# New layouts for the heads and tails of a decoder's feed-forward blocks, and for the opening of its sparse attention

## The chip, the cores and the metric

The kernel runs on one core of a Trainium2 chip. The metric is the device time of one execution in microseconds; lower is better. Runs of the kernel before gave 2072.43, 2068.01 and 2056.33 us, and their median is the time to compare with.

## What is computed

Two layers work on x (512 tokens of 1024 features, fp32). Each layer is a half-step gated feed-forward network (FFN), a mixer, and a second half-step FFN. The mixer of the first layer is a short gated convolution, that of the second is native sparse attention (NSA). Each of the six sub-layers starts from its own RMS norm with a shift and a scale, and its result is added to x through a gate. Shift, scale and gate come from the condition c. Cut to what matters:

```python
def adaln(x, g, shift, scale):
    return rms_norm(x, g) * (1 + scale[:, None, :]) + shift[:, None, :]

def swiglu(h, w_in, w_out):                        # 1024 -> 2 x 2816 -> 1024
    g, u = jnp.split(h @ w_in, 2, axis=-1)
    return (jax.nn.silu(g) * u) @ w_out

def short_conv_mixer(h, w_in, conv_w, w_out):      # 1024 -> 3 x 1024 -> 1024
    b_gate, c_gate, v = jnp.split(h @ w_in, 3, axis=-1)
    y = causal_conv_of_3(c_gate * v, conv_w)
    return (b_gate * y) @ w_out

def nsa_mixer(h, ...):     # 16 heads of 64, 4 groups of keys and values
    q, kc, vc, ks, vs, kw, vw, gl = jnp.split(h @ w_in, offs, axis=-1)
    q, k_sel, k_win = per-head rms_norm of q, ks, kw
    k_cmp = rms_norm(compress(kc)); v_cmp = compress(vc)   # blocks of 32, stride 16, gelu MLP
    out = sum over three branches of gate * softmax(q k^T + bias) v
    return out @ w_out
```

## The kernel before

**Data.** x lies transposed in SBUF: eight tiles x[d] of 128 features by 512 tokens. D is 1024, KD = 8 is the number of such tiles, T = 512, HT = 256; HALVES are the token columns 0 to 255 and 256 to 511. A matrix product has fp32 accuracy through three products: each operand is split into hi and lo (split, L165: ACT writes hi, then VectorE subtracts and writes lo), and mm3 (L169) adds hi x hi, hi x lo and lo x hi into one accumulator. So L170, L171 and L172 carry most of the matmuls, and L166 and L167 most of the splits. Weights are loaded as wraw by SP and split into whi and wlo (weights, L174). The default pool wp has three buffers of each; own gives another pool.

**Order.** The program is written stage by stage, and the tile scheduler puts each engine's instructions in an order by priority and dependence. Work under tc.high_priority() goes to the front of what is ready in its engine's order. At run time every engine then works strictly through its own list, and an instruction that waits holds all those behind it. SP issues loads, in its own order, and a load waits until the buffer that it writes is free.

**Stages**, with the microseconds of the profile: the first FFN, which also computes shifts, scales and gates (0 to 405), conv (to about 590), FFN2 (to 955), FFN3 (to 1314), NSA (to 1700), and FFN5 (to 2055).

**A norm.** Class Norm (L210) belongs to the sub-layer that it feeds. The residual of the sub-layer ahead adds to x[d], then square (L217) takes the square on ACT and sums it in nacc. When all eight d of a half are in, finish (L235) turns the sum by a matmul with ones into a column per token, takes the root in small VectorE steps (rsqrt, L192: eleven operations on 128x2 or 128x8), makes a diagonal dg (L249) and spreads it with another matmul pr (L250). Then piece (L293) makes h for one d and one half: xr = x * pr on VectorE (L297), hhi on ACT with scale and shift (L299), the full value hf or hfull by ACT (odd d, L302) or VectorE (even d, L304), and hlo as their difference on VectorE (L305).

**A head** is where a stage starts to use h piece by piece. head_start (L333) multiplies three weights with the first halves as the pieces come, then the fourth weight (L346 on), then the second halves in the same way. **A tail** (L359) is the end of a stage: its last outputs are computed in two halves of 256 columns, so that the norm of the first half can begin while the second is computed.

**FFN2, FFN3 and FFN5** use ffn (L460). The 22 hidden tiles come in three blocks (FOUR). For the first two hidden tiles the products are plain; the third is a plain pair; all later ones go through seven_products, a seven-multiplication scheme on 2 x 2 blocks. It needs four combinations t0 to t3 of quarters of hfull, split into th and tl (quarters, L307), and combinations qa and qb of the weight's quarters. p1 = the copy of its first product (L512); L518 to L524 combine the others into e, with the silu between, and keep splits e into ahi and alo. The last block's output products run over d = 0 and 1 in full width and over d = 2 to 7 in tail. Its weights come from in_ffo.

**conv** (L564) has three weights per output column tile: gate, value, b.

**NSA** (L639) starts with the compressor (L759): head_start over the key and value columns of the compressed branch, then sixteen ACT copies t (L779), the sum with positions flr (L788), its split flh and fll, the products ph, a gelu and a second product. Between those, natural (L658) makes queries and keys in natural layout (tokens on partitions) and normed gives each half its own root chain over 128x8. attend (L857) then goes through 32 units (group, head, branch) three deep. heads and keys turn queries and keys by transposes (pq and pk), table (L881) loads rows of the bias table by 32 issues of SP before the first unit, and the remaining projections are spread through the units. At the end the output projection of groups 2 and 3 loads four blocks er, splits them into eh and el, and adds its results in two halves.

**PSUM** has 8 banks. Before, every stage kind has its own layout: new_psum closes the pool and opens another with other tags (L64 to L75):

```python
BANKS = {"mm": 6, "pr": 2, "pre": 5, "pt": 3, "nat": 2, "s": 2, "t": 2, "o": 2}
def new_psum():
    nonlocal ps
    ps_stack.pop_all().close()
    ps = pool(ps_stack, "ps", 1, space=PSUM)
```

Of the kernel before, what the change touches and what calls it, by code (L numbers as in the profile page):

```python
# [11 lines left out]
F32 = mybir.dt.float32  # L12
F32R = mybir.dt.float32r
# [7 lines left out]
P = 128  # L21
# [12 lines left out]
NG = 4  # L34
# [17 lines left out]
def decoder_kernel(ctx, tc, xT, cT, ng, adaw, adab, ffi, ffo, cwi, cw, cwo,  # L52
# [13 lines left out]
    ps = None  # L66
    BANKS = {"mm": 6, "pr": 2, "pre": 5, "pt": 3, "nat": 2, "s": 2, "t": 2, "o": 2}

    def psum(name, tag="mm"):
        return ps.tile([P, T], F32, name=name, tag=tag, bufs=BANKS[tag])  # L70

    def new_psum():
        nonlocal ps
        ps_stack.pop_all().close()
        ps = pool(ps_stack, "ps", 1, space=PSUM)  # L75
# [98 lines left out]
    def weights(src, nk, ncol, own=None, held=3):  # L174
        def part(name, dt, bufs):
            return (own or wp).tile([P, nk * ncol], dt, name=name, tag=name, padded_shape=[P, KD * P], bufs=bufs)

        hi, lo = part("whi", F32R, held), part("wlo", F32R, held)
        raw = part("wraw", F32, 3 if own is None else 2)
# [30 lines left out]
    class Norm:  # L210
# [69 lines left out]
        def alloc(self, hp):  # L280
            self.full = None
            self.hi = [hp.tile([P, T], F32R, name=f"hhi{d}") for d in range(KD)]
            self.lo = [hp.tile([P, T], F32R, name=f"hlo{d}") for d in range(KD)]
# [3 lines left out]
        def alloc_seven(self, tt, tq):  # L287
            self.full = tq.tile([P, KD, T], F32, name="hfull")
            self.t = [tq.tile([P, KD // 2, HT], F32, name=f"t{j}") for j in range(4)]
# [3 lines left out]
        def piece(self, d, hf):  # L293
            a, b = HALVES[hf]
            sc, sh = mod(self.s, 0, d), mod(self.s, 1, d)
            xr = tmp("xr", HT, "xr")
            nc.vector.tensor_mul(xr, x[d][:, a:b], self.pr[hf][:, 0:HT])  # L297
            hi = self.hi[d][:, a:b]
            nc.scalar.activation(hi, xr, AF.Identity, scale=sc, bias=sh)  # L299
# [5 lines left out]
            nc.vector.tensor_tensor(self.lo[d][:, a:b], hf_, hi, ALU.subtract)  # L305

        def quarters(self):  # L307
            n = KD // 2
# [24 lines left out]
    def head_start(nrm, h, jobs, both=3):  # L333
        os = [psum("hs") for _ in jobs]

        def go(n, ks, a, b):
            for k in ks:
                w, wc, kw = jobs[n](k)
                project(os[n][:, a:b], w, wc, h, [(kw, k)], k == 0, k == KD - 1, a, b)

        with tc.high_priority():
            for d in range(KD):
                nrm.piece(d, 0)
        for k in range(KD):
            for n in range(both):
                go(n, [k], 0, HT)  # L346
        for n in range(both, len(jobs)):
            go(n, range(KD), 0, HT)
        for d in range(KD):
            nrm.piece(d, 1)  # L350
        for k in range(KD):
            for n in range(both):
                go(n, [k], HT, T)
        for n in range(both, len(jobs)):
            go(n, range(KD), HT, T)
        return os


    def tail(s, nrm, jobs, h, ahead):  # L359
        nxt = ahead() if ahead else None  # L360
        for a, b in HALVES:
            for d, w, wc, ks in jobs:
                o = psum("ty")
                project(o[:, 0:b - a], w, wc, h, ks, True, True, a, b)
                residual(s, d, o, nrm, a, b, True)
# [94 lines left out]
    def ffn(s, f, nrm, nxt, w0, ahead):  # L460
        with ExitStack() as es:
            hp = pool(es, "hp", 1)
            h = nrm.alloc(hp)
            in_es = es.enter_context(ExitStack())
            tt = pool(in_es, "tt", 1)
            swa = pool(in_es, "swa", 1)
# [780 lines left out]
```

## Time and profile before

| | us |
|---|---|
| runs | 2072.43, 2068.01, 2056.33; median 2068.01 |
| profiled execution: time | 2060.89 |
| its span, first to last instruction | 2058.8 |
| mean granted clock of TensorE in it | 0.988 |
| TensorE (PE) busy, 12404 matmuls | 1980.4 |
| VectorE (DVE) busy, 2634 instructions | 1505.2 |
| ScalarE (ACT) busy, 1361 instructions | 874.3 |
| GpSimd (POOL) busy, 395 instructions | 266.9 |

The page of the profile lists, by part, how busy each engine is, the chain that ended last, the costliest groups of instructions and the loads. A group's row names a line of the code, the engine, the tiles (out <- in), shape and count; then busy time, mean duration of one in ns, and the idle time of the engine just before them with what ended it. Matmuls overlap: one of 512 columns shows 0.39 to 0.40 us, while the next begins after 0.23. Waits are also answered by stretches of the span, and so are busy time and the granted clock.

### The profile page before, as it was taken

What the parts mean: (1) busy time and instruction counts of PE and PEld (TensorE: products, weight loads), DVE (VectorE), ACT (ScalarE), POOL (GpSimd) and SP (SyncE); (2) the same over time, 40 slices, a digit from 0 to 9 for tenths busy, and PEclk for the clock granted to TensorE, in tenths of its full rate; (3) what the DMA queues carried; (4) which work ended last, traced back from release to release, by engine and by line L of the source; (5) the groups of instructions that cost most, each with busy time, mean ns of one, the idle gap of its engine ahead of it and who ended that gap; (6) DMA issues with size and microseconds to landing.
All of it is one profiled execution on the core that took longest, in us unless ns stands there. A gap on an engine that the chain in (4) does not pass through costs nothing.

```text
span 2058.8 us, 32164 instructions
## 1 busy us (share of the span) xinstructions
PE 1980.4 (96%) x12404; PEld 1771.8 (86%) x12404; DVE 1505.2 (73%) x2634; ACT 874.3 (42%) x1361; POOL 266.9 (13%) x395
## 2 busy tenths in 40 slices
PE   5999999999999999998999999999999989999999
PEld 3878888888888899998889999898888788898988
DVE  8878888664477677677867677885887878675865
ACT  3322222332244343335534334554777856343432
POOL 0000000100011111110101111001344530111100
PEclk9999999999999999999999999999999999999999
DMA  8888988322234555552545555233111133465642
GB/s 308 301 309 320 330 308 322 126 92 82 92 96 125 144 149 156 149 159 59 154 134 151 156 139 143 100 103 94 52 47 28 41 98 96 134 164 151 164 114 81
DMA packets 110309, 307.37 MB, mean 149 GB/s; under 512 B 14795, under 2 KB 15067, under 8 KB 110156
## 3 DMA queue, kind: packets, MB, share of 16 engines
q1 hardware_dynamic: 88956, 259.86, 36.9%
q0 software_dynamic: 21200, 45.46, 11.3%
q8 instruction: 97, 1.59, 0.3%
q14 instruction: 56, 0.46, 0.1%
HBM read 302.12 MB, written 3.15 MB: 148 GB/s over the span
## 4 chain that ended last, share of the span: by engine, by line
PE 39%; DVE 7%; ACT 3%; issue 2%; SPq 1%; DMA 1%; POOL 0%; ACTq 0%; POOLq 0%; DVEq 0%
PE gu L170 6%; PE gu L171 6%; PE gu L172 6%; PE y L170 4%; PE y L172 4%; PE y L171 4%; DVE L L972 1%; DVE wlo L167 1%; PE nat L170 1%; PE nat L172 1%; PE nat L171 1%; PE s L962 1%; PE ty L172 1%; SPq L881 1%; PE ty L171 1%
## 5 line engine op out<-in xcount | busy, mean ns | idle before, releaser
L166 ACT ACTIVATE whi<-wraw 128x1024 fp32r<-128x1024 f32 (+2 forms) x292 | 291.1, 1000 | 587.8 <-PE y L171 249.7
L167 DVE TENSOR_TENSOR wlo<-wraw,whi 128x1024 fp32r<-128x1024 f32 (+2 forms) x292 | 335.3, 1151 | 66.0 <-ACT whi L166 63.8
L170 PE MATMUL gu<-hhi,whi 128*128 128x256 f32 (+1 forms) x808 | 265.8, 329 | 2.0 <-ACT whi L166 2.0
L171 PE MATMUL gu<-hlo,whi 128*128 128x256 f32 (+1 forms) x808 | 265.6, 329 | 0.0
L172 PE MATMUL gu<-hhi,wlo 128*128 128x256 f32 (+1 forms) x808 | 264.9, 328 | 0.0
L170 PE MATMUL y<-ahi,whi 128*128 128x512 f32 x611 | 241.1, 398 | 3.8 <-ACT ahi L166 3.8
L172 PE MATMUL y<-ahi,wlo 128*128 128x512 f32 x611 | 243.9, 399 | 0.0
L171 PE MATMUL y<-alo,whi 128*128 128x512 f32 x611 | 242.9, 398 | 0.4 <-DVE alo L167 0.4
L121 DVE CUSTOM_DVE_ANT_0 adaraw<-adaraw,cond 128x1024 f32<-128x1024 f32 x144 | 174.5, 1222 | 27.2 <-DMA adaraw<-in_adaw 25.4
L487 POOL DMA_DIRECT2D qa<-in_ffi x114 | 104.3, 1015 | 645.2 <-DMA qa<-in_ffi 542.9
L170 PEld LDWEIGHTS gu<-hhi,whi 128*128 128x128 f32 x808 | 152.1, 188 | 18.2 <-ACT whi L166 3.9
L171 PEld LDWEIGHTS gu<-hlo,whi 128*128 128x128 f32 x808 | 151.8, 188 | 14.4
L172 PEld LDWEIGHTS gu<-hhi,wlo 128*128 128x128 f32 x808 | 152.1, 188 | 14.0
L166 ACT ACTIVATE qbh<-qb 128x1536 fp32r<-128x1536 f32 x57 | 85.0, 1491 | 165.2 <-PE gu L171 143.9
L170 PEld LDWEIGHTS y<-ahi,whi 128*128 128x128 f32 x611 | 114.9, 189 | 36.5 <-ACT ahi L166 8.6
L554 DVE SCALAR_TENSOR_TENSOR x<-y,mods,x 128x512 f32<-128x512 f32 x72 | 54.0, 750 | 120.7 <-PE y L172 120.7
L171 PEld LDWEIGHTS y<-alo,whi 128*128 128x128 f32 x611 | 115.7, 189 | 29.2 <-DVE alo L167 0.8
L172 PEld LDWEIGHTS y<-ahi,wlo 128*128 128x128 f32 x611 | 115.6, 189 | 26.7
L170 PE MATMUL gu<-th,qah 128*128 128x256 f32 x456 | 129.8, 285 | 6.3 <-ACT p L512 6.3
L172 PE MATMUL gu<-th,qal 128*128 128x256 f32 x456 | 129.6, 284 | 0.0
L171 PE MATMUL gu<-tl,qah 128*128 128x256 f32 x456 | 129.5, 284 | 0.0
L172 PE MATMUL gu<-th,qbl 128*128 128x256 f32 x456 | 129.0, 283 | 0.0
(284 smaller groups left out, 5141.2 us busy)
## 6 DMA issues: line engine op xcount, KB each, us to landing
adaraw<-in_adaw SPq DMA_DIRECT2D x144, 512.0 KB, 5.9
wraw<-in_ffi SPq DMA_DIRECT2D x119, 512.0 KB, 4.5
qa<-in_ffi SPq DMA_DIRECT2D x114, 256.0 KB, 4.1
qa<-in_ffi POOLq DMA_DIRECT2D x114, 256.0 KB, 5.3
wraw<-in_ffo SPq DMA_DIRECT2D x72, 384.0 KB, 4.2
qb<-in_ffi POOLq DMA_DIRECT2D x57, 256.0 KB, 3.3
wraw<-in_cwi SPq DMA_DIRECT2D x24, 512.0 KB, 3.3
wraw<-in_ffo SPq DMA_DIRECT2D x20, 512.0 KB, 4.4
```

Source lines behind the costliest of these rows:

```text
L121: nc.vector.tensor_tensor_reduce(out=raw, in0=raw, in1=cond, scale=1.0, scalar=0.0, op0=ALU.mult, op1=ALU.add, accum_out=m)
L166: nc.scalar.activation(hi, src, AF.Copy)
L167: nc.vector.tensor_tensor(lo, src, hi, ALU.subtract)
L170: nc.tensor.matmul(o, sh, mh, start=first, stop=False)
L171: nc.tensor.matmul(o, sh, ml, start=False, stop=False)
L172: nc.tensor.matmul(o, sl, mh, start=False, stop=last)
L487: nc.gpsimd.dma_start(qa[:, i], quart(1, 0), accum_op=ALU.add)
L554: nc.vector.scalar_tensor_tensor(x[d], o, mod(s, 2, d), x[d], op0=ALU.mult, op1=ALU.add)
L881: nc.sync.dma_start(tb[NR * e:NR * (e + 1), q, :], src)
L962: nc.tensor.matmul(sps[:, off:off + n], Q[q][:, i * P:(i + 1) * P], m[:, 0:n], start=(e == 0), stop=(e == 1))
L972: nc.vector.tensor_tensor_reduce(out=Ls[u][:, LOFF[i]:LOFF[i] + n], in0=sps[:, off:off + n], in1=tb[:, q, T - n:T], scale=1.0, scalar=3e38 ...
```

## The change

- *PSUM.* One pool for the whole kernel. The tag mm takes the banks of nat, s and t in turn; pr, po, pht, pk and pg go with o. Each of these four tags has two banks. No pool is closed between stages.
- *Pieces.* The scale goes into the first product, and the shift into the last: two scalar_tensor_tensor on VectorE and one ACT operation for each piece. hfull is kept without the shift, and quarters first adds it with eight ACT operations of 512 columns.
- *Heads.* head_start runs all its weights through the first half, then all through the second. The conv head takes a fourth weight (the first of d = 1), the FFN heads put the fourth weight in a pool hw of its own, whose memory the tiles t use afterwards, and the compressor does the same with the value weights.
- *FFN tails.* All eight outputs of the last block run in halves. The first three of four hidden tiles of six outputs come first, then the fourth tile. The weights of d = 4 to 7 go into tiles of th, tl and qa that are free by then. Residuals in the tail have high priority.
- *NSA's opening.* The raw query or key projection is copied to SBUF; a group's two halves share one root chain over 128x16 and are multiplied in place. The t copies write a layout that flr reads in order. Queries and keys of group 0 are turned during the opening. natural's evacuations no longer have high priority.
- *NSA's end.* The four output blocks are loaded and split during units 25, 26, 28 and 29, into memory of h.

The core of the diff:

```diff
+    ps = pool(ctx, "ps", 1, space=PSUM)
+    six = cycle(("nat", "s", "t"))
     def psum(name, tag="mm"):
-        return ps.tile([P, T], F32, name=name, tag=tag, bufs=BANKS[tag])
+        tag = next(six) if tag == "mm" else {"pr": "o"}.get(tag, tag)
+        return ps.tile([P, T], F32, name=name, tag=tag, bufs=2)
...
-            nc.vector.tensor_mul(xr, x[d][:, a:b], self.pr[hf][:, 0:HT])
+            nc.vector.scalar_tensor_tensor(xr, x[d][:, a:b], sc, self.pr[hf][:, 0:HT], op0=ALU.mult, op1=ALU.mult)
-            nc.scalar.activation(hi, xr, AF.Identity, scale=sc, bias=sh)
-            hf_ = tmp("hf", HT) if self.full is None else self.full[:, d, a:b]
-            if d % 2:
-                nc.scalar.activation(hf_, xr, AF.Identity, scale=sc, bias=sh)
-            else:
-                nc.vector.tensor_scalar(hf_, xr, sc, sh, op0=ALU.mult, op1=ALU.add)
-            nc.vector.tensor_tensor(self.lo[d][:, a:b], hf_, hi, ALU.subtract)
+            nc.scalar.activation(hi, xr, AF.Identity, bias=sh)
+            nc.vector.scalar_tensor_tensor(self.lo[d][:, a:b], xr, sh, hi, op0=ALU.add, op1=ALU.subtract)
...
+    def head_start(nrm, h, jobs):
+        os = [psum("hs") for _ in jobs]
+        for hf, (a, b) in enumerate(HALVES):
+            with tc.high_priority():
+                for d in range(KD):
+                    nrm.piece(d, hf)
+            for k in range(KD):
+                for o, job in zip(os, jobs):
+                    w, wc, kw = job(k)
+                    project(o[:, a:b], w, wc, h, [(kw, k)], k == 0, k == KD - 1, a, b)
...
-                nrm.alloc_seven(tt, pool(tq_es, "tq", 1))
-                os = head_start(nrm, h, [(lambda k, w=w_: (w, 0, k)) for w_ in w])
+                nrm.alloc_seven(pool(tq_es, "tf", 1))
+                with ExitStack() as hw_es:
+                    hw = pool(hw_es, "hw", 1)
+                    w = w0 + [weights(ffi[f, j, c], KD, P, hw, 1, wp) for j, c in js[len(w0):]]
+                    os = head_start(nrm, h, [(lambda k, w=w_: (w, 0, k)) for w_ in w])
+                nrm.alloc_sums(tt, pool(tq_es, "tq", 1))
                 os += pair(f, nj, h)
                 nrm.quarters()
...
+            early = [(d, psum("ty")) for d in range(6)]
+            for d, o in early:
+                part(o, d, range(n - 1), 0, HT)
+            for d, o in early:
+                part(o, d, range(n - 1, n), 0, HT)
+                with tc.high_priority():
+                    residual(s, d, o, nxt, 0, HT, True)
+            for d, t in [(d, 0) for d in range(6, KD)] + [(d, HT) for d in range(KD)]:
+                o = psum("ty")
+                part(o, d, range(n), t, t + HT)
+                with tc.high_priority():
+                    residual(s, d, o, nxt, t, t + HT, True)
...
-                    r = rsqrt(v, 8)
-                    nc.vector.tensor_tensor(dst[hf].rearrange("p t (a b) -> p (t a) b", b=HD), o..., r..., ALU.mult)
+                    nc.scalar.activation(dst[hf].rearrange("p t c -> p (t c)"), o, AF.Copy)
+            def normed(dst, v):
+                nc.vector.tensor_scalar(v, v, 1.0 / HD, EPS, op0=ALU.mult, op1=ALU.add)
+                r = rsqrt(v, 16)
+                for i, t in enumerate(dst):
+                    t = t.rearrange("p t (a b) -> p (t a) b", b=HD)
+                    nc.vector.tensor_tensor(t, t, r[:, 8 * i:8 * i + 8, None].to_broadcast([P, 8, HD]), ALU.mult)
...
-                next(c0)
-                run(queries(0))
+                q0 = natural(0, raw(query_tiles(0), vq))
+                run(q0)
+                next(c0)
+                normed(qn[0], vq)
                 next(c0)
...
+                heads(0, 0)
                 g = gates(es2, h, gsb)
                 next(g)
                 next(c0, None)
+                heads(0, 1)
                 v1 = natural(7, values(vn[1]))
                 run(v1[:1])
+                keys(0, 0)
...
+            ew = []
+            for i, v in enumerate((25, 26, 28, 29)):
+                needed[v].append(lambda i=i: ew.append(last_weight(i)))
```

More of the change, by code (lines that the diff above doesn't have):

```diff
@@ L718, in begin @@
                 def begin():
-                    qn[g] = [na.tile([P, 2, CW], F32, name=f"qn{g}{hf}", tag="qn", bufs=3) for hf in range(2)]
-                    return normed(qn[g])
+                    dst, v = query_tiles(g), squares()
+                    return raw(dst, v), lambda: normed(dst, v)
                 return steps(g, begin)
             def value_steps():
-                return steps(9, lambda: values(vn[0]))
+                return steps(9, lambda: (values(vn[0]), lambda: None))
             def run(jobs):
```

297 lines of the change are left out of this document (139 added, 158 removed).

## The prediction

> **What bounds the kernel now.** The page comes first. TensorE (PE) is busy for 96% of the span and the largest part of the chain that ended last; no other engine comes near.
>
> ```profile
> span 2058.8 us, 32164 instructions
> PE 1980.4 (96%) x12404; PEld 1771.8 (86%) x12404; DVE 1505.2 (73%) x2634; ACT 874.3 (42%) x1361; POOL 266.9 (13%) x395
> PE 39%; DVE 7%; ACT 3%; issue 2%; SPq 1%; DMA 1%; POOL 0%; ACTq 0%; POOLq 0%; DVEq 0%
> ```
>
> So a change gains only by removing matmul work or the holes between matmuls. To price the work I read the matmul starts in the timeline, 512 columns first, then 256.
>
> ```profile
> 859.74 0.39 PE L171 MATMUL y<-alo,whi 128*128 128x512 f32 x1
> ...
> 862.54 0.39 PE L171 MATMUL y<-alo,whi 128*128 128x512 f32 x1
> ...
> 600.30 0.28 PE L172 MATMUL hs<-hhi,wlo 128*128 128x256 f32 x1
> ...
> 600.77 0.28 PE L172 MATMUL hs<-hhi,wlo 128*128 128x256 f32 x1
> ```
>
> Twelve intervals in 2.80 us make 0.233 us for 512 columns, four in 0.47 make 0.118 for 256. To find the holes I read the table by stretches around every place that the diff touches. After from:to stand the length, the busy time of each engine, and PEclk, the granted clock (1.00 is full speed).
>
> ```profile
> core 0: us, PE busy (x) PEld busy (x) DVE busy (x) ACT busy (x) POOL busy (x), PEclk, DMA share, GB/s
> 398.00:430.00 32.00, 29.59 (x214) 28.03 (x215) 24.95 (x80) 18.64 (x33) 0.00 (x0) 0.95 0.15 50
> 600.00:630.00 30.00, 28.62 (x171) 25.16 (x170) 27.86 (x39) 20.46 (x28) 0.00 (x0) 0.94 0.25 84
> 640.00:660.00 20.00, 17.06 (x131) 16.86 (x130) 16.13 (x20) 9.34 (x12) 3.57 (x5) 0.91 0.64 149
> 925.00:945.00 20.00, 16.52 (x104) 14.84 (x103) 12.54 (x20) 7.07 (x12) 2.16 (x2) 0.91 0.54 149
> 1320.00:1335.00 15.00, 11.71 (x68) 10.45 (x67) 12.98 (x40) 9.85 (x16) 0.00 (x0) 0.77 0.19 70
> 1413.00:1440.00 27.00, 22.06 (x152) 19.72 (x150) 14.53 (x34) 13.92 (x30) 5.62 (x13) 0.91 0.29 79
> 1440.00:1660.00 220.00, 204.73 (x1358) 183.06 (x1358) 180.40 (x532) 165.58 (x412) 102.48 (x183) 0.96 0.18 51
> 1660.00:1680.00 20.00, 15.52 (x95) 13.10 (x96) 14.02 (x27) 11.45 (x23) 7.60 (x12) 0.91 0.42 102
> ```
>
> A hole thus costs twice: once as idle time, and again as (1 - PEclk) times the stretch. At 1320-1335 the second part alone is 0.23 x 15 = 3.4 us. Who was waited for stands in PE's waits, asked stretch by stretch (in order: the conv head, FFN2's head, FFN2's tail, attention's normed head, the compressor, the start of attention, its tail; us in all, times, longest):
>
> ```profile
> PE hs L170 <- ACT hhi L299: 1.4, 2, 1.1
> PE pr L250 <- DVE dg L249: 1.0, 1, 1.0
> ...
> PE gu L170 <- ACT p L512: 2.9, 1, 2.9
> ...
> PE y L170 <- ACT ahi L166: 3.5, 1, 3.5
> ...
> PE hs L170 <- ACT hhi L299: 1.4, 1, 1.4
> PE pr L250 <- DVE dg L249: 0.8, 1, 0.8
> ...
> PE ph L171 <- DVE wlo L167: 1.2, 1, 1.2
> ...
> PE pq L874 <- DVE vn L167: 2.7, 2, 2.3
> PE s L962 <- DVE st L972: 1.0, 1, 1.0
> PE pc L917 <- DVE k L891: 0.9, 1, 0.9
> ...
> PE ty L170 <- ACT eh L166: 3.0, 1, 3.0
> ```
>
> **The change part by part.** Gains carry a plus. Bounds stand in brackets.
>
> *Matmul shapes.* Read off the two instruction orders, 96 matmuls of 512 columns become 192 of 256: 96 x (2 x 0.118 - 0.233) = 0.3 us lost, and some more for accumulators that start and end twice. I take -1 [-2, 0].
>
> *Conv head.* All four accumulators now go through the first column half before any piece of the second, so one half lasts 4 x 8 x 3 x 0.118 = 11.3 us, where three took 8.5. The norm chain of the second half (pr, eleven small root steps, dg) hides under it. The pieces lose a DVE and half an ACT operation each, 0.41 and 0.29 us, so VectorE no longer keeps pace with PE at the margin. Waits of 2.4 us and 0.05 x 32 = 1.6 of clock go. I leave half a microsecond: +3.5 [0, +4].
>
> *FFN tails.* In FFN2's tail one wait of 3.5 us stands. ACT had the split of a late in_ffo block in its queue ahead of ahi, and the block came late. The new tail issues 6 x 3 x 3 = 54 products of the first three k of six outputs (6.4 us) ahead of the last hidden tile. The chain from the last product to that tile is four operations like
>
> ```profile
> L522 DVE TENSOR_TENSOR e<-gu,e 128x512 f32<-128x512 f32 x57 | 39.4, 692 | 5.9
> ```
>
> with a shorter one, silu and ahi, some 4.2 us in all. It fits under the 54 products, and so does the second half's norm under 96 first-half products. Without this cover the 3.5 would stand. The weights for d = 4 to 7 go into idle t and qa tiles, whose loads are issued early. Wait 3.5 and clock 0.09 x 20 = 1.8 go: +5 [0, +5.3]. FFN3's and FFN5's tails show no such hole and gain nothing here.
>
> *FFN heads.* The rows that price them:
>
> ```profile
> L170 PE MATMUL gu<-th,qah 128*128 128x256 f32 x456 | 129.8, 285 | 6.3 <-ACT p L512 6.3
> L167 DVE TENSOR_TENSOR wlo<-wraw,whi 128x1024 fp32r<-128x1024 f32 (+2 forms) x292 | 335.3, 1151 | 66.0 <-ACT whi L166 63.8
> L167 DVE TENSOR_TENSOR tl<-t,th 128x1024 fp32r<-128x1024 f32 x12 | 14.1, 1216 | 0.0
> L166 ACT ACTIVATE qbh<-qb 128x1536 fp32r<-128x1536 f32 x57 | 85.0, 1491 | 165.2 <-PE gu L171 143.9
> L170 PE MATMUL hs<-hhi,whi 128*128 128x256 f32 (+1 forms) x352 | 93.6, 313 | 10.0 <-ACT hhi L299 4.6 <-ACT hhi L277 3.5 <-ACT whi L166 1.8
> L171 PE MATMUL hs<-hlo,whi 128*128 128x256 f32 (+1 forms) x352 | 106.1, 313 | 1.7 <-DVE hlo L305 1.1
> L172 PE MATMUL hs<-hhi,wlo 128*128 128x256 f32 (+1 forms) x352 | 103.8, 306 | 2.7 <-DVE wlo L167 2.7
> ```
>
> Before, the three heads lose 6.3 us to p. They lose 4.6 less the two 1.4 above, or 1.8, to hhi; 1.8 to whi; 0.06 x 30 + 0.09 x 20 = 3.6 to the clock; and of the 3.8 for hlo and wlo I give them 1.7, the first FFN and attention having the rest: 15.2. In the new order the t tiles lie where the fourth weight lay, so the sums t cannot start until the last hs product is done. The next pair's splits also come only then. VectorE's queue behind that point is three wlo (3.5), four sums t (one input tile of the size of tl, so the same 1.2: 4.9) and four tl (4.9): 13.2 us, with qal and qbl (3 us) behind. ACT's qbh and then the copy of p1 come out at about 17 us. TensorE has the pair, 48 x 0.233 = 11.2, and two products that need no t, 24 x 0.118 = 2.8, and a little more: 14.4. So a new wait of about 3 us stands in each head, 9 in all. In 640-660 the wait of 2.9 us brought the clock to 0.91, or 1.8 us; the other heads share 6.3 - 2.9 = 3.4, two shorter waits, and I saw no dip behind these. I count the clock for half of the new ones: 15.2 - 9 - 3 = +3 [-15, +12]. The lower end is every block of the new wp queue late by 3 us with the clock, the upper no new wait.
>
> By the Trainium skill, "TensorE: Matmul & The Clock Gate", section "HAM oscillation — how this bites in real kernels", only idle gaps above about 3.4 us bring the clock down. By that rule none of the three new waits would, and the forecast would be 3 us lower. This trace does not agree: in 398-430 no listed wait exceeds 1.1 us, and the clock was 0.95.
>
> *Attention's normed head.* The same as in the conv: 2.2 us of waits in the rows above, a share of those for hlo and wlo, 3.4 of clock; the cover is again 11.3 us of products. +6 [0, +6.8: 1.2 of that share].
>
> *Attention's opening.* Before, the compressor's first two accumulators were done early, and 144 narrow products stood behind. Now all four end together, and only 24 products of natural layout (2.9 us) stand in PE's queue ahead of ph, which needs flh. ACT has all sixteen t copies ahead of flh:
>
> ```profile
> L779 ACT ACTIVATE t<-hs 64x256 f32<-64x256 f32 x16 | 6.1, 379 | 2.3 <-PE hs L172 2.1
> L205 DVE SCALAR_TENSOR_TENSOR rs_r<-rs_b,rs_r 128x8 f32<-128x8 f32 (+3 forms) x48 | 8.8, 184 | 0.9
> ```
>
> 16 x 0.38 = 6.1, then one split (1024 columns, two thirds of qbh: 1.0): 7.1 - 2.9 = 4.2 us of new wait. The old 1.2 at ph is given back, and three root chains of eleven such 0.2-us steps. I take -2.5 [-8, +2].
>
> *Start of attention.* The first bias-table loads still wait for the same values and are all issued by SP one after another:
>
> ```profile
> 1413.53 15.40 SPq L881 DMA_DIRECT2D tb<-tbl  x32
> ```
>
> 15.4 us, and with the time from issue to landing (its own issue is the first 0.4 of it)
>
> ```profile
> DMA to landing us min/median/max: 1.7/1.9/3.6
> ```
>
> 1.4 more: 16.8. The transposes of the first heads and keys now lie ahead of it, which takes out the 2.7 at pq and 0.9 at pc. Behind stand pk, six s and 96 products of natural layout (0.5 + 1.1 + 11.6 = 13.2), so 3.6 is left at s, with 1.7 of clock like 925-945. Before it was 4.6 of waits and 0.09 x 27 = 2.4. +2 [-2, +7].
>
> *Rest of attention.* 0.04 x 220 = 8.8 us is clock, and the waits are many and short, most for VectorE, which is busy 180 of 220. Three root chains (2.2 us each) leave it; raw copies of 512 columns come in on ACT, two for each joined chain, under cover of ACT's 54 free us. Four more weight splits come near the end, at 1.0 and 1.15 us; the lower bound is these eight not hidden, less what the chains save. I take +5 [-4, +13].
>
> *Attention's tail.* The eh split wait (3.0) and 0.09 x 20 of clock go, because these weights are split during attention. About 1.2 for osum's own split stays: +4 [0, +5].
>
> **Sum.** -1 + 3.5 + 5 + 3 + 6 - 2.5 + 2 + 5 + 4 = 25 us. The profiled execution took 2060.9 us (span 2058.8), so it would come to about 2036. The median of the three runs is 2068.0, 7 above; against it the forecast is 2043.
>
> **The rivals.**
>
> *The new waits eat the gain.* The head waits come to 4.5 us with the clock each time (18.6 against 15.2: -3.4), the opening pays 4.2 and two clock dips (-7), and the start and rest of attention gain nothing. -1 + 3.5 + 5 - 3.4 + 6 - 7 + 0 + 0 + 4 = 7: 2061. For it: TensorE had least slack in just these heads. Against: the waits are worked out from an order in which VectorE never runs ahead.
>
> *All holes close.* No new wait in the heads (+12), the opening +2, attention's start +7 and rest +13, conv +4, tail +5.3, normed head +6.8, tail +5: 55, so 2013. For it: the cover in heads is 14.4 of 17. Against: the table loads cannot come earlier than SP issues them.
>
> *Slower.* A split in the queues of ACT and VectorE, ahead of work that TensorE needs, waits for a block whose load SP could issue only after an older split had freed its buffer. FFN2's tail shows it once already, at 3.5 us. A load lands in
>
> ```profile
> wraw<-in_ffi SPq DMA_DIRECT2D x119, 512.0 KB, 4.5
> ```
>
> 4.5 us, and the two splits make 6.7; with 1.7 of clock, 8.4 for each exposed block. The new order has 15 such blocks: in each FFN head the fourth weight and the two of the pair (9), two in the opening, four inside attention. Three exposed ones cancel the gain, (2089 - 2043) / 8.4 = 5.5 make it 1% slower; with seven it is 2102. Against: PE's waits name a late load behind only one hole now, and three raw buffers remain.
>
> **How the numbers follow.** The forecast has 0.45, the eaten gain 0.27, closed holes 0.16, slower 0.12. About 1% (20.7 us) is what a measurement here tells from no change. Of the forecast's 0.45 some 0.07 lies above 2047, so faster is 0.16 + 0.38 = 0.54, same 0.27 + 0.07 = 0.34, slower 0.12. The range is 2010 to 2076: the low end is the closed holes, the upper one the eaten gain with two exposed blocks (2061 + 2 x 8.4 = 2078, cut to 2076).
>
> **What would show it.** Right: no wait for ahi after the early products of FFN2's tail, no dg wait in the conv and attention heads, PEclk 1.00 in these places and in attention's tail; a wait of 2 to 4 us on th, tl or p1 some 14 us after each FFN head, and one of about 4 on flh ahead of the first ph. Wrong: waits on whi or hfull inside the heads, or DVE idle on DMA there. If s still waits for st at attention's start, the tables were the bound.

## The result, and the profile after

The changed kernel takes 2043.4 us (median of 14 runs, 2039.9 to 2051.7), the kernel before, run beside it, 2061.4 us. The ratio of the two, run by run, is 0.9924 with a 95% interval from 0.9908 to 0.9939: 0.76% faster, or some 18 us by the medians. That lies inside the 1% which the prediction called no change and gave 0.34 (faster had 0.54), and inside its range; the forecast time was 2043.0. The experiments below show that this agreement comes from errors that cancel: the schedule gave 7 to 8 us of the 25 forecast, a cause that the prediction did not have gave the rest of the 18, and the median of 2068 from which the 25 were taken was 7 us too high.

The page of the changed kernel, profiled in an execution of 2051.7 us: span, engines, chain. Line numbers from here on are those of the kernel profiled, so that L168 is L170 of the kernel before.

```profile
span 2049.9 us, 32209 instructions
PE 1970.3 (96%) x12500; PEld 1765.1 (86%) x12500; DVE 1486.0 (72%) x2532; ACT 870.1 (42%) x1361; POOL 266.8 (13%) x393
PE 24%; DVE 5%; ACT 2%; issue 2%; DMA 1%; POOL 0%; DVEq 0%; ACTq 0%; POOLq 0%
```

TensorE bounds it as before; 96 matmuls were added, as forecast, and its busy time still fell by 10 us. The table by stretches, at the places of the change (length, busy time of PE, PEld, DVE, ACT, POOL, then the granted clock):

```profile
410.00:435.00 25.00, 24.73 (x200) 24.35 (x201) 16.74 (x52) 9.97 (x21) 0.00 (x0) 1.00 0.14 43
592.00:622.00 30.00, 27.91 (x208) 26.60 (x208) 16.64 (x47) 14.17 (x26) 4.17 (x5) 0.94 0.33 64
625.00:657.00 32.00, 26.22 (x170) 24.33 (x169) 27.02 (x31) 16.45 (x22) 4.68 (x6) 0.89 0.52 125
925.00:955.00 30.00, 28.69 (x234) 28.01 (x233) 24.69 (x60) 11.76 (x24) 3.56 (x4) 1.00 0.53 139
955.00:1015.00 60.00, 56.17 (x407) 52.82 (x406) 47.43 (x81) 33.26 (x49) 4.68 (x6) 0.97 0.33 85
1300.00:1336.00 36.00, 35.19 (x292) 34.46 (x291) 29.79 (x85) 15.92 (x31) 0.00 (x0) 1.00 0.13 39
1336.00:1352.00 16.00, 8.54 (x58) 8.05 (x57) 4.95 (x5) 13.64 (x20) 0.00 (x0) 0.80 0.34 121
1400.00:1440.00 40.00, 38.08 (x317) 36.98 (x316) 22.73 (x54) 21.65 (x49) 9.11 (x18) 1.00 0.30 81
1640.00:1680.00 40.00, 39.59 (x282) 35.53 (x282) 30.26 (x83) 27.96 (x69) 15.77 (x27) 1.00 0.17 53
```

The conv head (410-435), FFN2's tail (925-955), attention's normed head (1300-1336), the start of attention (1400-1440) and its tail (1640-1680) now run at full clock with TensorE nearly always busy. The heads of FFN2 and FFN3 (592-657 and 955-1015) and attention's opening (1336-1352) do not. What TensorE waits for there, from PE's waits over the whole span (us in all, times, longest; a wait of 13.4 us at the start of the kernel, 13.1 before, is left out):

```profile
PE gu L168 <- ACT p L499: 8.5, 3, 4.3
PE ph L168 <- ACT flh L831: 7.3, 1, 7.3
PE y L168 <- ACT ahi L164: 7.0, 4, 2.8
...
PE gu L168 <- ACT qbh L164: 2.2, 3, 0.7
PE pr L249 <- DVE dg L248: 2.2, 2, 1.9
PE gu L170 <- DVE wlo L165: 1.7, 3, 0.6
PE pq L900 <- DVE qn L712: 1.5, 1, 1.5
```

p, ahi and flh make 22.8 us. A tabulation of the trace's matmul starts shows where the time went. A stage is counted from its first hs product to the next stage's. "Holes" are the parts of the intervals above the usual 0.231 us (after a matmul of 512 columns) or 0.1175 us (256), counted where an interval is over 6% longer; times in us. Two executions of the changed kernel stand here, the second with a clock of 0.994 where the first had 0.986:

| | first FFN | conv | FFN2 | FFN3 | NSA | FFN5 |
|---|---|---|---|---|---|---|
| before: stage | 405.4 | 183.8 | 366.6 | 358.3 | 385.5 | 355.3 |
| after: stage | 410.3 | 181.7 | 362.0 | 360.5 | 375.1 | 356.4 |
| after again: stage | 406.4 | 181.7 | 360.9 | 357.9 | 370.9 | 354.7 |
| before: holes | 19.3 | 6.0 | 17.8 | 9.4 | 45.6 | 7.2 |
| after: holes | 20.5 | 2.0 | 17.3 | 15.9 | 39.0 | 12.5 |
| after again: holes | 16.0 | 2.0 | 16.2 | 13.3 | 38.7 | 10.9 |

Conv and attention gained in holes. The two executions of the changed kernel differ by 5.3 us in the holes of the three later FFNs, so a smaller difference between single executions says little. In these three FFNs holes grew from 34.4 to 45.7 or 40.4 us, and yet FFN2 became shorter: what is left when the holes are taken out, the plain run of matmuls, fell by some 4 us in each of them (348.8 to 344.7 in FFN2). That is no part of the schedule, and it was tested first.

### The profile page after: what moved, and what is told of

The parts are those of the page before. It is cut to its first block, busy times and chain, and to the rows that moved or that the text cites. A ratio compares the mean times of both kernels' runs of the same rounds, so it can differ in the third digit from the quotient of the medians.

```text
span 2049.9 us, 32209 instructions
## 1 busy us (share of the span) xinstructions
PE 1970.3 (96%) x12500; PEld 1765.1 (86%) x12500; DVE 1486.0 (72%) x2532; ACT 870.1 (42%) x1361; POOL 266.8 (13%) x393
## 5 line engine op out<-in xcount | busy, mean ns | idle before, releaser
L164 ACT ACTIVATE whi<-wraw 128x1024 fp32r<-128x1024 f32 (+2 forms) x286 | 284.6, 999 | 578.6 <-PE y L169 242.9
L165 DVE TENSOR_TENSOR wlo<-wraw,whi 128x1024 fp32r<-128x1024 f32 (+2 forms) x286 | 329.2, 1154 | 89.4 <-ACT whi L164 86.6
L168 PE MATMUL gu<-hhi,whi 128*128 128x256 f32 (+1 forms) x808 | 265.1, 328 | 1.2 <-ACT whi L164 0.6
L170 PE MATMUL gu<-hhi,wlo 128*128 128x256 f32 (+1 forms) x808 | 262.6, 327 | 1.7 <-DVE wlo L165 1.7
L168 PE MATMUL y<-ahi,whi 128*128 128x512 f32 x587 | 232.2, 398 | 7.1 <-ACT ahi L164 7.0
L169 PE MATMUL y<-alo,whi 128*128 128x512 f32 x587 | 233.9, 399 | 0.7 <-DVE alo L165 0.7
L170 PE MATMUL y<-ahi,wlo 128*128 128x512 f32 x587 | 232.9, 398 | 0.0
L168 PEld LDWEIGHTS gu<-hhi,whi 128*128 128x128 f32 x808 | 151.8, 188 | 19.6 <-ACT whi L164 2.5
L170 PEld LDWEIGHTS gu<-hhi,wlo 128*128 128x128 f32 x808 | 151.2, 188 | 17.5 <-DVE wlo L165 2.3
L168 PEld LDWEIGHTS y<-ahi,whi 128*128 128x128 f32 x587 | 110.5, 189 | 38.6 <-ACT ahi L164 11.5
L541 DVE SCALAR_TENSOR_TENSOR x<-y,mods,x 128x512 f32<-128x512 f32 x72 | 54.0, 750 | 118.1 <-PE y L170 118.1
L168 PE MATMUL gu<-th,qah 128*128 128x256 f32 x456 | 130.6, 286 | 8.5 <-ACT p L499 8.5
L169 PEld LDWEIGHTS y<-alo,whi 128*128 128x128 f32 x587 | 111.3, 190 | 28.4 <-DVE alo L165 2.2
L170 PEld LDWEIGHTS y<-ahi,wlo 128*128 128x128 f32 x587 | 111.5, 190 | 25.9
L168 PE MATMUL gu<-th,qbh 128*128 128x256 f32 x456 | 127.8, 281 | 2.2 <-ACT qbh L164 2.2
L170 PE MATMUL gu<-th,qal 128*128 128x256 f32 x456 | 129.7, 284 | 0.0
```

The source lines that it names most:

```text
L164: nc.scalar.activation(hi, src, AF.Copy)
L165: nc.vector.tensor_tensor(lo, src, hi, ALU.subtract)
L168: nc.tensor.matmul(o, sh, mh, start=first, stop=False)
L169: nc.tensor.matmul(o, sh, ml, start=False, stop=False)
L170: nc.tensor.matmul(o, sl, mh, start=False, stop=last)
L541: nc.vector.scalar_tensor_tensor(x[d], o, mod(s, 2, d), x[d], op0=ALU.mult, op1=ALU.add)
```

## The experiments

### The rate of matmuls and where the operands lie

The table by stretches, 720-748 in FFN2 and the gu products alone, first before, then after. TensorE is busy all the time and the clock is 1.00 in both:

```profile
720.00:748.00 28.00, 28.00 (x237) 28.00 (x237) 5.86 (x10) 1.10 (x3) 1.00 0.76 192
```

```profile
720.00:748.00 28.00, 28.00 (x243) 28.00 (x242) 7.50 (x12) 1.09 (x3) 1.00 0.78 191
```

The same 28 us hold 243 matmuls instead of 237: one in 115.2 ns instead of 118.1. The edit removes tiles and adds tiles, so nearly all SBUF addresses move. I took both operands' addresses from the compiled programs and put them beside the trace's intervals. What the interval goes with is the distance between the two operands' addresses, modulo 128 bytes. To test it, tiles that nothing uses were added, which shift only the addresses.

**e1_before_q64**: the kernel before, with 64 bytes ahead of the qa tiles.

```diff
+            sw.tile([P, 16], F32, name="pad")
```

> The kernel before, with one unused tile of 64 bytes per partition ahead of the weight combinations qa and qb of the seven-product scheme, so that these lie 64 bytes further; nothing else moves. Placement theory (the time from one matmul to the next depends on the distance of its two operands' SBUF addresses modulo 128 bytes: 120 ns at 0, 117 to 118 at 32 or 96, 114 at 64, for 256 columns): 3420 matmuls go from distance 0 to 64, 3420 x 5.7 ns = 19 us faster than before, about 2042. Holes theory (only waits and clock made the difference, and the shorter intervals of the changed kernel come from its other PSUM layout or from another load beside it): no change, within 0.3% of before.

2040.2 us, against 2059.5 for the kernel before beside it: 0.9924 [0.9904, 0.9944]. That is 19.3 us where the counting had 19. One unused tile gives the old kernel the whole ratio of the change.

**e2_after_h32**: the changed kernel with 32 bytes ahead of h, which puts the operands of the FFNs' seven products back at the distances of before.

```diff
+            hp.tile([P, 8], F32, name="pad")
```

> The changed kernel, with one unused tile of 32 bytes per partition ahead of h in the three later FFNs, which brings back the distances of the kernel before there (q combinations to th and to h: 0; first weights to h: 96). Placement theory: the 4788 products go from a mean of 116.4 to 119.2 ns, 13 us slower than the changed kernel, about 2056, so that little is left of the gain over before. Holes theory: as the changed kernel, 2043.

2055.1 us, 0.9981 [0.9967, 0.9995]: nearly all of the gain is gone.

**e3_after_phases**: the changed kernel with four such pads, chosen for short intervals.

```diff
+    ap.tile([P, 8], F32, name="pad", bufs=1)
...
+                self.fa.tile([P, 24], F32, name="pad", bufs=1)
...
+                tt.tile([P, 16], F32, name="pad")
...
+            sw.tile([P, 16], F32, name="pad")
```

> The changed kernel with four unused tiles of 32 to 96 bytes, in the pools of the first stages' weights, of the hidden tiles, of qa/qb and of th/tl, so that 512-column products have operands at distance 0 and 256-column products at distance 64 wherever one pad reaches them. Placement theory: seven-product matmuls 116.4 to 114.3 (10 us), output products of 512 columns 233 to 228 (9 us), first FFN and conv 231 to 227.5 (6 us), tails' th/tl products (1.6 us): about 26 us, so 2017. Holes theory: 2043.

2030.0 us, 0.9864 [0.9842, 0.9887]. That is 8.6 us under the changed kernel beside it (e0 below), where the counting had 26. The table below shows what came short: the products of t came to 117.8 ns instead of some 114, and those of conv and the first FFN went only to 229.9.

The same stretch in e1, e2 and e3:

```profile
720.00:748.00 28.00, 28.00 (x247) 28.00 (x246) 7.43 (x12) 1.10 (x3) 1.00 0.81 204
```

```profile
720.00:748.00 28.00, 28.00 (x236) 28.00 (x235) 7.45 (x12) 1.10 (x3) 1.00 0.74 180
```

```profile
720.00:748.00 28.00, 28.00 (x244) 28.00 (x243) 7.50 (x12) 1.00 (x3) 1.00 0.80 201
```

247, 236 and 244: the rate follows the pads while the schedule stays. The mean interval by product, and in brackets the distance in bytes:

| products | before | after | e1 | e2 | e3 |
|---|---|---|---|---|---|
| 256 columns, t with qa or qb | 119.8 (0) | 117.0 (32) | 115.6 (64) | 119.9 (0) | 117.8 (64) |
| 256 columns, h with qb | 120.0 (0) | 119.4 (0) | 115.5 (64) | 120.1 (0) | 114.4 (64) |
| 256 columns, h with w | 118.3 (96) | 114.2 (64) | 118.4 (96) | 119.8 (96) | 114.6 (64) |
| 512 columns, conv's cv | 226.7 (0) | 228.1 (0), 233.3 (96) | 226.7 (0) | 228.2 (0), 233.3 (96) | 229.9 (0) |
| 512 columns, FFN's y | 233.3 (96) | 228.4 (0), 233.4 (96) | 233.4 (96) | 228.6 (0), 233.4 (96) | 227.9 (0) |

For the change this makes 2736 x 2.8 + 1368 x 4.1 ns = 13.3 us gained in the seven products. In conv and the first FFN half of the products moved to distance 96: 696 x 6.6 ns, or 4.6 us lost. Another 1 us is lost on the other half and 1 gained where a part of y moved from 96 to 0. The products nat in attention, which the table leaves out, also gained: 576 of them moved from distance 32 to 64, from 117.4 to 114.7 ns, or 1.6 us.

### The whole change again

**e0_after_again**: no edit.

> The changed kernel once more, beside the others on the same chip. Both theories: about 2043, 0.992 of before; a second look at its waits, which should again have flh (7 us) at attention's opening, p (some 8 us in three heads) and ahi (some 7) as the longest.

2038.6 us, 0.9910 [0.9888, 0.9932]. e2 differs from it almost only in the seven products' distances, and the medians are 16.4 us apart: a little more than the 13.3 counted. So the change less its luck with addresses is e2's 4 us, and some 3 more for the distances that conv and the first FFN lost and nat gained, which e2 leaves in place: 7 to 8 us. This is an estimate; e2's interval alone leaves 1 to 7 us for its part.

### Attention's opening

In the changed kernel ph waits 7.3 us for flh, where the prediction had 4.2. The tile t's answer, before and then after (duration ns: min/median/max):

```profile
L779 ACT ACTIVATE t<-hs x16: 376/379/383, 1339.2 to 1348.2; 64x256 f32<-64x256 f32 x16
...
L788 DVE TENSOR_TENSOR flr<-t,poss x4: 2083/2140/2192, 1342.3 to 1370.4; 128x992 f32<-128x992 f32 x4
```

```profile
L820 ACT ACTIVATE t<-hs x16: 591/602/642, 1337.1 to 1346.5; 64x256 f32<-64x256 f32 x16
...
L830 DVE TENSOR_TENSOR flr<-t,poss x4: 1181/1185/1194, 1342.2 to 1367.3; 128x992 f32<-128x992 f32 x4
```

The new layout of t makes VectorE's read contiguous, at 1185 ns instead of 2140, and ACT's write strided, at 602 instead of 379. Sixteen writes stand ahead of the first flh: 16 x 0.223 = 3.6 us later. The step of the write is now 128 bytes, that of the old read was 32. The Trainium skill, "SBUF — State Buffer", section "Door 1: The DMA port swizzle (why `[64,N]` ≈ `[32,N]`)", says that SBUF is read and written in lines of 16 bytes and that every access which crosses to a new line pays; the two durations agree.

**e10_old_t_layout**: t as before, read with the old step; a single run.

```diff
-                t2 = cm.tile([P, NG, 8, 32], F32, name=f"t2{kv}")
+                t2 = cm.tile([P, NG, T // 2], F32, name=f"t2{kv}")
...
```

> The changed kernel with the t copies written in the layout of the kernel before, so that flr reads with a stride again. If the strided write made each copy 0.62 instead of 0.38 us: sixteen copies 3.8 us shorter, flr 2.1 instead of 1.2 us but beside the copies, the wait for flh 3 to 4 us instead of 7.3 (the prediction had 4.2). Rival: the copy is slow because four banks are read at once or for another reason: 0.6 us and 7 us stay.

2034.0 us, one run without an interval. PE's waits:

```profile
PE ph L168 <- ACT flh L830: 3.6, 1, 3.6
```

The copies take 379 ns again, and the wait is 3.6, near the 4.2 that was worked out from that duration; so the strided write is the cause, and not that four banks are read. NSA's holes are 32.8 us instead of 38.7.

**e4_v_on_dve**: the eight value copies on VectorE, the eight key copies on ACT.

```diff
-                            nc.scalar.activation(t2[...], ov[...], AF.Copy)
+                            if kv:
+                                nc.vector.tensor_copy(dst, src)
+                            else:
+                                nc.scalar.activation(dst, src, AF.Copy)
```

> The changed kernel with the eight t copies of the value half on VectorE instead of ScalarE; the eight of the key half stay. If the new wait at attention's opening is ScalarE's queue of sixteen copies (0.62 us each with the new strided write) ahead of flh: the wait for flh falls from 7.3 to about 3.6 us, its clock loss with it, 4 to 6 us faster than the changed kernel, about 2036. Rival: the w1 splits behind flh or fll end last anyway, and the wait comes back under another name: no change.

2038.9 us, 0.9897 [0.9876, 0.9918]: no difference from e0 (0.9910). PE's waits, 1320 to 1365:

```profile
PE nat L168 <- ACT whi L164: 3.4, 1, 3.4
PE ph L168 <- ACT flh L835: 0.4, 1, 0.4
```

7.3 became 0.4, but a split of a later weight in ACT's queue now ends 3.4 us late. About half of the wait is left under another name; the 4 to 6 us that were expected do not show in the time.

### The waits inside the FFNs

ACT's timeline in the changed kernel, at the end of FFN3's first block, shows the wait for ahi arise (start, duration, in brackets the idle time before):

```profile
1025.09 1.06 ACT L164 ACTIVATE qah<-qa 128x1024 fp32r<-128x1024 f32 x1 [5.96 <-DMA qa<-in_ffi]
1026.06 0.61 ACT L510 ACTIVATE e<-e 128x512 f32<-128x512 f32 x1
```

ACT stands 6 us at the split of a qa block that has not landed; the silu of the last hidden tile (L510) waits behind it, and ahi behind that.

**e6_silu_first**: silu, the product behind it and its split at high priority.

```diff
+                with tc.high_priority():
                     nc.scalar.activation(e[:, 0:2], e[:, 0:2], AF.Silu)
                     ...
                     keep(e[:, 0:2].rearrange("p a b -> p (a b)"))
```

> The changed kernel with silu, its product and the splits into ahi and alo at high priority in the seven-product scheme, so that ScalarE's queue has them ahead of a qah split whose block arrives late. If the new ahi waits (7 us in all, 2.8 at the end of the first block in FFN3 and FFN5) come from a qah split that holds silu behind it: ahi waits fall to about 2 us, 5 us faster than the changed kernel, about 2036. Rival: the qa blocks then reach the products later, and p or qbh waits take it: no change or up to 3 us slower.

2039.5 us, 0.9894 [0.9873, 0.9915]. The wait for ahi goes from 7.0 (7.7 in e0) only to 4.1 us, where 2 was expected, and p remains at 7.8. The 5 us expected do not show against e0's 0.9910.

**e7_three_waits**: e4 and e6 together, and the first qa splits of a head ahead of other work.

```diff
+                with ahead_of(j < 5):
                     split(qa, ah_, al_)
```

> The last two edits together, and the first two qah splits of each later FFN at high priority, which frees qa for the third block's load earlier. Waits theory: flh 3.6, ahi 2, p from 8 to about 5: 12 us faster than the changed kernel, about 2029. Rival (late loads only move from one name to the next): within 4 us of the changed kernel.

2031.9 us, 0.9859 [0.9835, 0.9883]. The waits for p are gone; 3.5 for qbh and 6.6 for ahi remain, and 1.8 for qbl and 1.4 for sg are new. Against e4 and e6 this is some 7 us.

**e8_waits_phases**: e7 with the four pads of e3.

> The same with the four pads of the third run. If placement and waits are independent, their gains add: 12 + 10 us faster than the changed kernel, about 2019, 0.981 of before. If shorter products only make the late loads later, the waits grow by what the intervals save, and it is about 2028.

2018.4 us, 0.9788 [0.9763, 0.9813]. The pads take 13.5 us off e7; alone, in e3 against e0, they took 8.6. The shorter products did not make the waits grow by what they save.

### The order and the memory of the FFN heads

**e9_old_ffn_heads**: only the FFN heads as before: in each half three weights first and then the fourth, which comes from wp, and memory of their own for t. Pieces, tails and the operands' distances stay. The last argument of head_start is how many weights go through a half together.

```diff
...
-                with ExitStack() as hw_es:
-                    hw = pool(hw_es, "hw", 1)
-                    w = w0 + [weights(ffi[f, j, c], KD, P, hw, 1, wp) for j, c in js[len(w0):]]
-                    os = head_start(nrm, h, [(lambda k, w=w_: (w, 0, k)) for w_ in w])
-                nrm.alloc_sums(tt, pool(tq_es, "tq", 1))
+                nrm.alloc_sums(tt, tq)
+                w = w0 + [ffn_in(f, j, c) for j, c in js[len(w0):]]
+                os = head_start(nrm, h, [(lambda k, w=w_: (w, 0, k)) for w_ in w], 3)
```

> The changed kernel with the FFN heads of the kernel before: the fourth weight again in the shared pool and after the other three in each half, and the t tiles in memory of their own. Distances of the seven-product operands stay as in the changed kernel. If the new heads cost what the stage times say (FFN3 and FFN5 some 5 us longer than before once the distances are put back, and FFN2 as much, hidden by its tail's gain of 5): wlo and qbh waits in the heads go, p waits fall from 8 to about 6, and it is 8 to 15 us faster than the changed kernel, about 2029. Rival: the extra time in FFN3 and FFN5 is the late qah ahead of silu at the end of the first block, which this edit leaves: within 3 us of the changed kernel.

2025.6 us, 0.9833 [0.9805, 0.9861]; the whole change in e0 had 0.9910. So the new heads cost some 0.8%, 13 us by the medians. The holes of FFN2, FFN3 and FFN5 are 9.0, 8.6 and 8.2 us, 25.8 against 40.4 in e0: 14.6. Two of its groups:

```profile
L168 PE MATMUL gu<-th,qah 128*128 128x256 f32 x456 | 129.5, 284 | 8.0 <-ACT p L500 8.0
...
L168 PE MATMUL y<-ahi,whi 128*128 128x512 f32 x587 | 230.2, 395 | 1.2 <-ACT ahi L164 1.2
```

The waits of gu for qbh and wlo and of pr for dg are gone, and that for ahi is 1.2 instead of 7.0. But p stays: 8.0 us, where 6 was expected and the changed kernel has 8.5 and 7.6 in its two executions. With t in memory of its own, and its sums begun during the head, the wait for p is as long, so it is not what the new heads cost.

**e12_order_only**: only the order of the products as before; the fourth weight's pool and the memory of t stay as changed, and so do the distances of the seven products.

```diff
-                    os = head_start(nrm, h, [(lambda k, w=w_: (w, 0, k)) for w_ in w])
+                    os = head_start(nrm, h, [(lambda k, w=w_: (w, 0, k)) for w_ in w], 3)
```

> The changed kernel with only the order of the FFN heads put back (three weights through a half, then the fourth), while the fourth weight keeps its own pool and the t tiles still lie in that memory. Putting back both order and memory gave about 2026. Memory theory (the sums t, and behind them the first qah split and the third block's reload, are late because the t tiles must wait for the last hs product): as the changed kernel, 2038 to 2043, with wlo, qbh and ahi waits as there. Order theory (four interleaved accumulators end together, so that the pair and the first silus come late): about 2026, and those waits gone.

2029.4 us, 0.9858 [0.9826, 0.9889]; the holes of the three FFNs are 12.6 + 10.1 + 9.2 = 31.9. By holes, some 8.5 us of the 14.6 come from the order and 6.1 from the memory that t shares; but each is one execution, two executions of the same kernel were 5.3 apart, and by the ratios e9 and e12 are not apart. How the cost divides stays open; it is neither of the two results that the run was to tell apart. The timeline of FFN3's head shows what each does. First the changed kernel, then e9, then e12: the first product of the head, the first sum t and the first split of the next qa.

```profile
953.99 0.73 PE L168 MATMUL hs<-hhi,whi 128*128 128x256 f32 x4 [1.26 <-ACT hhi L300]
...
980.28 1.22 DVE L310 TENSOR_TENSOR t<-hfull 128x1024 f32<-128x1024 f32 x1
...
991.60 1.05 ACT L164 ACTIVATE qah<-qa 128x1024 fp32r<-128x1024 f32 x1
```

```profile
942.15 0.62 PE L168 MATMUL hs<-hhi,whi 128*128 128x256 f32 x3 [0.77 <-ACT hhi L300]
...
956.85 1.22 DVE L310 TENSOR_TENSOR t<-hfull 128x1024 f32<-128x1024 f32 x1
...
970.18 1.05 ACT L164 ACTIVATE qah<-qa 128x1024 fp32r<-128x1024 f32 x1
```

```profile
947.72 0.74 PE L168 MATMUL hs<-hhi,whi 128*128 128x256 f32 x4 [1.26 <-ACT hhi L300]
...
971.89 1.22 DVE L310 TENSOR_TENSOR t<-hfull 128x1024 f32<-128x1024 f32 x1
...
978.85 1.05 ACT L164 ACTIVATE qah<-qa 128x1024 fp32r<-128x1024 f32 x1
```

From the head's start to the sums it is 26.3, 14.7 and 24.2 us, to the split 37.6, 28.0 and 31.1. The changed head holds the raw weight buffers and VectorE for longer; the split of qa, and with it the release of its buffer and the next load, comes 9.6 us later, and the end of the first block pays for it, in the wait for ahi above. That chain is read from the order of the rows; for it speaks that in e9 and e12, where the split comes earlier, the wait is 1.2 us and 0.1. In e12 p costs 12.4 us instead:

```profile
L168 PE MATMUL gu<-th,qah 128*128 128x256 f32 x456 | 131.5, 288 | 12.4 <-ACT p L500 12.4
```

### All together

**e11_best**: e9, the three edits of e7 and the four pads.

> The old FFN heads, the three edits against waits and the four pads together. If all are independent: 2018 (waits and pads together) less the 10 us of the heads, about 2008, 0.974 of before. If the old heads and the earlier qah splits cure the same wait: about 2014.

2001.8 us (1995.5 to 2006.0), 0.9703 [0.9677, 0.9729]: some 60 us faster than before and 40 faster than the change, and below both expectations. By the ratios the gains add up: e8's 0.9788 less the 0.0077 between e0 and e9 is 0.9711. One row of PE's waits:

```profile
PE nat L169 <- ACT whi L165: 3.4, 1, 3.4
```

The waits for p and flh are gone and ahi's are 0.6 us; the split that replaced flh's wait is still there.

## Why the prediction was right or wrong

*The time* was right, its reasons only in part. The forecast took 25 us from a median of 2068; later runs put that median at 2061.4. The schedule gave 7 to 8 us, near the rival in which the new waits eat the gain (7 us). The addresses gave the other 10 or so. That the sum hit 2043 within half a microsecond is luck.

*The sum's step at the FFN heads failed; it is the largest error.* The term was +3 with a lower bound of -15, and e9 against e0 gives -14.6, at the bound. The delay named, t behind the last hs product, is there: the sums start 26.3 us after the head instead of 14.7. But what it was to cost is not: p has 8.5 us in three waits where 9 were forecast, which looks like a hit, and it has 8.0 in e9 without that delay. So the 6.3 us that p cost before did not go, though the sum took them off, and no new wait behind the sums t shows beside them; what p waits for in all these kernels stays open. Missing in the sum were the waits for qbh, wlo and dg (6.1 together), and above all the late qa split at the end of the first block (ahi, 7.0). Of that the prediction had the mechanism, under *slower*: a split in ACT's queue for a late load ahead of work that TensorE needs. The blocks that it named, the fourth weight and the pair, were not the exposed ones; a later qa was, at the end of the first block, at up to 2.8 us of wait instead of 8.4 with the clock. A third qa buffer, which would let that load start earlier, was not tried.

*FFN2's tail* was right: no wait for ahi remains in 925-955, the clock is 1.00, and with the old heads (e9) FFN2's holes are 8.8 us fewer than before, the shorter pieces among their causes.

*Conv head:* +3.5 forecast, holes 6.0 to 2.0, so +4 measured, no dg wait left. In e1 the old schedule has 4.5, without the dip of the clock, so some 2.5 is the schedule's. The stage became only 2.1 us shorter, since half of its cv products moved to distance 96. *Attention's normed head* and *tail:* the waits are gone and the clock is 1.00 as foreseen; their sizes cannot be told apart.

*Opening:* the mechanism was right, the copy's price was not. The prediction kept 379 ns for a write whose layout it had said would change; it was 602, and the wait 7.3 us. e10 gives 3.6 at the old price.

*Start of attention:* +2 forecast with 3.6 us left at s. PE's waits from 1400 to 1440 in the changed kernel are these two, so that the cover was longer than counted:

```profile
PE nat L168 <- DVE k L910: 1.2, 1, 1.2
PE pt L1044 <- POOL L L1035: 0.7, 1, 0.7
```

Attention as a whole was forecast at 6 - 2.5 + 2 + 5 + 4 = 14.5 us, and its stage became 10.4 or 14.6 us shorter in the two executions, 6.6 or 6.9 of it by holes; some 1.6 is nat's distance, and the rest was not taken apart.

*Matmul shapes:* the prediction took 0.233 and 0.118 us from one place each and used them for the changed kernel. The row above has 115.2 ns. This step, that an interval read before holds after, is the second one that failed, with the opposite sign.

*The clock:* the sum priced it as a share of a stretch, read once for each place. In 592-622 of the changed kernel the trace lists waits of 1.9 and 0.2 us and a clock of 0.94; after 7.3 us it was 0.80. By the Trainium skill, "TensorE: Matmul & The Clock Gate", section "HAM oscillation — how this bites in real kernels", gaps below about 3.4 us would not have done the first. The dip is there, but it does not come back. In e0 the same stretch has waits of 2.1 and 0.2 us and a full clock. In e1, the old schedule, the conv head has the waits that the prediction priced, 1.4 and 1.0 us, and a full clock where the kernel before had 0.95. First e0, then e1:

```profile
588.00:618.00 30.00, 27.69 (x215) 26.30 (x214) 17.99 (x48) 14.52 (x28) 4.18 (x5) 1.00 0.35 76
```

```profile
398.00:430.00 32.00, 29.58 (x217) 27.66 (x217) 27.05 (x81) 20.06 (x34) 0.00 (x0) 1.00 0.18 64
```

FFN2's head in e1 waits 3.0 us for p, where the prediction had 2.9 and a clock of 0.91, and has 1.00 as well. So the clock terms of these heads, 1.6 and 3.6 us, belong to the execution that was profiled, and the waits alone do not bring them. At the opening the dip came back in e0 (0.79 after 7.3 us).

## What to carry to other kernels

Before a gain of about 1% is credited to a schedule, shift the addresses with an unused tile, in the old kernel too: here 64 bytes were worth as much as the whole change. When a head is reordered, follow the buffers it holds to their next use: the price came some 70 us later, as a load that could not be issued in time and a split that stood ahead of an unrelated silu. A layout change that saves one engine's strided read can hand a strided write to another, as it did here, and the one on the waited-for chain decides. A dip of the clock in one profile is not yet a cost of the wait beside it: look whether it comes back in a second execution.

## What was not expected of the hardware

The interval of fp32 matmuls at full clock goes with the two operands' addresses modulo 128 bytes. With 256 columns it is 119.4 to 120.1 ns at distance 0, 117.0 at 32, 118.3 to 119.8 at 96, and at 64 anything from 114.2 to 117.8 (115.6 in e1; 114.4 for h and 117.8 for t in e3). With 512 columns it is about 233.3 at 96 and 226.7 to 229.9 at 0. Three things stay open: why it is so; what decides at 64; and why conv and the first FFN at distance 0 take 226.7 ns in the kernel before and 229.9 in e3, so that this part of e3 did not give what the counting promised. That the addresses are the cause is shown by the pads for the seven products and for y; that their distance is what counts, and not also each operand's own place, is a reading of addresses beside the trace, and the spread at 64 and at 0 says that it is not all.

The clock records of these traces hold two values only, 1.00 and 0.50. Each dip lasts 3.41, 6.83 or 10.24 us (one that the end of a trace cuts off aside), so that it costs up to 1.7, 3.4 or 5.1 us. The profiled execution of the changed kernel had 13 dips before its end, 58 us in all; e0, the same kernel, had 6, 24 us in all, and its span was 13.4 us shorter.
